# A hybrid decoder step on one core: another order for the pieces ahead of the feed-forward products, other weights with low parts by DMA, other preparation leads

## The chip, the core and the metric

The kernel runs on one core of a Trainium2 chip. The core has a TensorE (PE, matmuls; its weight loads are shown apart as PEld), a VectorE (DVE), a ScalarE (ACT), a GpSimd (POOL) and a SyncE (SP), which here only issues DMAs. The metric is the device time of one execution in microseconds (us), the median of several.

## The reference

One layer of a decoder trunk for 1024 prompt tokens and 8 sample tokens that share the weights, all in fp32. Two mixers share one input projection: a pooling mixer (means over trailing windows 2, 4, 8, 16) and a convolution mixer (gated, 31 taps, layer norm, swish). Then come cross attention over 256 memory tokens (the prompt makes keys and values, the samples read caches), SwiGLU and a final norm.

```python
def pool_mixer(a_ext, start_pos, w_map, b_map, scale):
    ...
        win_sum = cg[:, POOL_HIST + 1:] - cg[:, POOL_HIST + 1 - w: POOL_HIST + 1 - w + L]
        outs.append(win_sum / cnt - af[:, POOL_HIST:, sl])
    ...
def mem_kv(mem, g_mem, w_k, w_v):
    m = rmsnorm(mem, g_mem)
    k = (m @ w_k).reshape(B, N_MEM, MEM_HEADS, MEM_HEAD_DIM)
    v = (m @ w_v).reshape(B, N_MEM, MEM_HEADS, MEM_HEAD_DIM)
    return k, v
def layer(...):
    h = rmsnorm(x, g_mix)
    u = h @ w_in
    a = u[..., :POOL_WIDTH]
    val = u[..., POOL_WIDTH:POOL_WIDTH + CONV_CH]
    gate = u[..., POOL_WIDTH + CONV_CH:]
    glu = val * jax.nn.sigmoid(gate)
    ...
    x = x + jnp.concatenate([ya, yb], axis=-1) @ w_out
    x = x + cross_attn(rmsnorm(x, g_attn), mk, mv, w_q, w_o)
    h = rmsnorm(x, g_ffn)
    x = x + (jax.nn.silu(h @ w_gate) * (h @ w_up)) @ w_down
```

## The kernel before

**Tiling.** Everything is kept transposed: 1024 channels are 8 blocks of 128 partitions, and the 1032 tokens are the free dimension (even prompt tokens, odd ones, samples), cut in 3 chunks of 344 for matmuls. An fp32 product is three fp32r matmuls of high and low parts (`PASSES`), so every weight block and every operand is first split in two: high part = a rounded copy, low part = value minus high part.

**Splits.** `split` (L367) makes the high part on ACT (L375) or POOL (L377) and the low part by a subtraction on DVE or POOL (L386). `split_by_dma` (L392), used for the weight blocks that `BY_DMA` names, makes the high part on ACT (L397) or POOL (L399), writes its negative in the low part's place in the same way, and POOL issues a DMA that reads the weight block again from memory and adds it there (L404). A weight block is loaded to a `raw` slot by SP (L361; 3 slots), and its two parts go to a `w` slot or, for the names in `WIDE`, to an `op` slot. A weight's preparation is put in the plan as many blocks ahead of its use as `LEAD` says (`w_take`, L461).

**What sets the order.** The kernel's functions only record tasks: engines that could do it, a cost for each, tiles read and written. `Program.order` (L146) then lays them out once, when the program is built: again and again it issues the task that can start first by the planner's own costs, and among those that tie the one with the lowest number, if a slot is free in its pools (`op` 19 slots, `scr` 3, `raw` 3, PSUM `mm` and `ms` 2 each, and others). Each engine gets its instructions as one fixed queue. On the chip an engine then works through its queue, and waits where an input isn't there.

**The pieces.** The numbers of the tasks follow the string `ORDER` (L41) up to the last operands of the feed-forward products. A letter is a piece and the digit its part: `g`, `v` gate and value products of the convolution mixer, `A` input products of the pooling mixer, `C`, `D`, `s` the convolution's sums, `W` windows (L806: doubling sums L821 to L826, mean L833 to L835), `n`, `m` the memory's norm and split, `K` keys (L850, PSUM tile kps, copied by DVE as kf at L861), `V` values (L925, PSUM tile vps, copied by ACT as vf at L939), `M` the pooling mixer's map (L871, PSUM tile pmap, which waits for the window tile win and a free PSUM tile; its copy is yf, split to opa), `L` layer norm, `O` and `B` the two halves of the output projection (PSUM oa and ob, weights w_out_a and w_out_b), `t` squares, `q` queries, `S`, `T`, `P` scores, transposed probabilities (pT) and their products with values (pv, copied by DVE as oo, L1096) of the prompt's attention, `a` to `e` the samples' attention (sample scores ss at L1143 from DVE's products at L1130; qd and pd are their queries and probabilities, which go through memory), `o` its output projection (po), and `u`, `x`, `y`, `z`, `h`, `r`, `i`, `j` the second norm, the feed-forward operand blocks, and the first of its weights. Weights are loaded and prepared in the order in which these pieces take them.

**Behind the pieces** come the feed-forward products (22 tiles, PSUM tile pr, L1336), the last blocks (`fd`, L1678) and the final norm. In `BY_DMA` only `w_dn` and `w_dn2` belong to them.

## Time and profile before

| | us |
|---|---|
| median of 3 runs (lowest, highest) | 1222.66 (1222.16, 1227.87) |
| the profiled execution: its own time | 1224.5 |
| its span in the trace | 1222.6 |
| TensorE busy | 1198.6 |
| DVE busy | 931.0 |
| mean granted TensorE clock | 0.996 |

The span is the time from the first to the last recorded instruction; the execution's own time holds in addition what lies around it. In the rows that the prediction quotes, times are us from the span's start; a timeline row has start, length, engine, line, operation, tiles and shapes, and in brackets the idle time ahead of it with what ended it. "x6" is the number of instructions in the row.

Where pieces stand in the profiled execution: input products to about 148, keys and values from 148.30, layer norm behind 215, output projection, queries from 302, the prompt's and samples' attention to 453, its output projection from 452.96 and the feed-forward products from 544.

### The profile page before, as it was taken

Reading aid. Unit: us, or ns where it says so; the run is one execution under the profiler, and the core shown is the slowest. Engines: PE = TensorE matmul, PEld = TensorE weight load, DVE = VectorE, ACT = ScalarE, POOL = GpSimd, SP = SyncE. Lnnn points to the kernel's source line nnn. Section 1 sums busy time; section 2 is a strip of 40 time slices with the busy share of each in tenths; the row PEclk is TensorE's granted clock in tenths of the full one; section 3 lists DMA queues with packets and bytes.
Section 4 is the critical chain, followed back from the end, with each engine's and each line's share of the span. In section 5 each row is a group of like instructions: output and inputs, shape, how many; then the busy total and the mean of one; then the engine's idle time right before and its main releaser. Section 6 shows DMA issues by size and latency. Waiting matters only on the chain.

```text
span 1222.6 us, 19409 instructions
## 1 busy us (share of the span) xinstructions
PE 1198.6 (98%) x7720; PEld 1122.5 (92%) x7720; DVE 931.0 (76%) x1558; ACT 519.8 (43%) x712; POOL 248.1 (20%) x294
## 2 busy tenths in 40 slices
PE   7999999999999999999999999999999999999997
PEld 7999987999999979998999999999999999999886
DVE  7899998655359876679877787777867798889754
ACT  7665656354124543454222222232232355444533
POOL 3587761224101002122000000000000023331101
PEclk9999999999999999999999999999999999999999
DMA  7235567433475775531322232222313597678512
GB/s 287 68 73 125 133 213 238 130 112 131 156 264 177 236 264 174 139 104 53 130 103 74 110 116 105 100 83 105 122 70 104 195 317 222 168 191 224 142 48 92
DMA packets 60314, 180.21 MB, mean 147 GB/s; under 512 B 7808, under 2 KB 11584, under 8 KB 58944
## 3 DMA queue, kind: packets, MB, share of 16 engines
q1 hardware_dynamic: 53824, 157.92, 36.8%
q0 software_dynamic: 6400, 21.06, 9.6%
q8 instruction: 60, 0.98, 0.3%
q14 instruction: 30, 0.25, 0.1%
HBM read 145.18 MB, written 33.78 MB: 146 GB/s over the span
## 4 chain that ended last, share of the span: by engine, by line
PE 81%; DVE 10%; DMA 4%; issue 2%; ACT 2%; POOL 1%; SPq 0%; DVEq 0%; POOLq 0%; ACTq 0%
PE pr L1336 48%; PE po L487 7%; PE ps L487 7%; PE fd L1678 6%; PE oa L487 4%; PE ob L487 4%; DVE cacc L691 3%; POOL y L674 1%; PE sc L1033 1%; DVE spcache_k L1130 1%; PE psv L487 1%; PE psg L487 1%; DMA spcache_k<-in_cache_k 1%; DMA raw<-in_w_out_a 1%; DVE w L386 1%
## 5 line engine op out<-in xcount | busy, mean ns | idle before, releaser
L1336 PEld LDWEIGHTS pr<-ab,wTb 128*128 128x128 f32 x1056 | 132.2, 188 | 3.6
L1336 PE MATMUL pr<-ab,wTa 128*128 128x260 f32 x1056 | 133.7, 282 | 0.1
L1336 PE MATMUL pr<-ab,wTb 128*128 128x260 f32 x1056 | 133.4, 282 | 0.0
L1336 PEld LDWEIGHTS pr<-ab,wTa 128*128 128x128 f32 x1056 | 131.0, 188 | 2.3 <-DVE su L1352 0.3
L1336 PE MATMUL pr<-ab,wG 128*128 128x512 f32 x528 | 129.3, 393 | 0.0
L1352 DVE TENSOR_TENSOR su<-pr,su 128x520 f32<-128x520 f32 (+1 forms) x112 | 77.6, 694 | 58.0 <-PE pr L1336 57.8
L1336 PEld LDWEIGHTS pr<-ab,wG 128*128 128x128 f32 x528 | 96.2, 188 | 19.6 <-DVE wG L386 0.4
L487 PE MATMUL ps<-xop,w 128*128 128x344 f32 x720 | 114.1, 320 | 0.0
L487 PEld LDWEIGHTS ps<-xop,w 128*128 128x128 f32 x720 | 113.6, 188 | 0.0
L1336 PEld LDWEIGHTS pr<-hb,dV 128*128 128x128 f32 x768 | 98.5, 188 | 3.9
L1336 PE MATMUL pr<-hb,dV 128*128 128x260 f32 x768 | 99.7, 283 | 0.0
L487 PE MATMUL ps<-xq,w 128*128 128x344 f32 x576 | 94.7, 321 | 0.0
L487 PE MATMUL po<-oo,w 128*128 128x344 f32 x576 | 91.2, 320 | 0.0
L487 PEld LDWEIGHTS po<-oo,w 128*128 128x128 f32 x576 | 90.9, 188 | 0.2 <-issue 0.2
L487 PEld LDWEIGHTS ps<-xq,w 128*128 128x128 f32 x576 | 90.7, 188 | 0.1
L691 DVE SCALAR_TENSOR_TENSOR cacc<-glu,vec,cacc 128x511 f32<-128x511 f32 (+14 forms) x116 | 77.4, 737 | 0.0
L1336 PE MATMUL pr<-hb,dW 128*128 128x512 f32 x288 | 73.9, 393 | 0.0
L1678 PE MATMUL fd<-ho,w 128*128 128x260 f32 (+1 forms) x432 | 69.2, 321 | 1.0 <-DVE x L1352 1.0
L375 ACT ACTIVATE w<-raw 128x1024 fp32r<-128x1024 f32 (+1 forms) x34 | 31.9, 941 | 90.0 <-issue 28.1
L1678 PEld LDWEIGHTS fd<-ho,w 128*128 128x128 f32 x432 | 61.8, 188 | 8.2 <-issue 1.9
L1363 POOL MEMSET su<- 128x16 f32 x22 | 2.4, 111 | 319.9 <-PE pr L1336 268.6
L1336 PE MATMUL pr<-ab,wU 128*128 128x512 f32 x264 | 64.8, 394 | 0.0
(306 smaller groups left out, 2178.1 us busy)
## 6 DMA issues: line engine op xcount, KB each, us to landing
gr<-in_w_gu SPq DMA_DIRECT2D x44, 512.0 KB, 3.6
hb<-su SPq DMA_DIRECT2D x8, 1040.0 KB, 4.2
hs<-hb SPq DMA_DIRECT2D x16, 520.0 KB, 4.3
dr<-in_w_dn SPq DMA_DIRECT2D x16, 512.0 KB, 7.4
spcache_k<-in_cache_k SPq DMA_DIRECT2D x12, 512.0 KB, 4.0
hs<-hb SPq DMA_DIRECT2D x12, 512.0 KB, 7.8
raw<-in_w_in SPq DMA_DIRECT2D x10, 512.0 KB, 3.6
hb<-he SPq DMA_DIRECT2D x8, 520.0 KB, 3.8
```

The costliest lines, as they stand in the source:

```text
L375: e.activation(dst(0), src(), AF.Copy, scale=1.0 if gain is None else gain)
L386: e.tensor_tensor(dst(1), src(), f32(dst(0)), ALU.subtract)
L487: e.matmul(ps[:, c, :CW], w[:, wi, cols], x[:, xi, c * CW : (c + 1) * CW], start=first and p == 0, stop=last and p == 2)
L674: add({"Pool": pool_tt(HALF), "DVE": dve(HALF)}, lambda e: e.tensor_tensor(yb[:, i, HALF + n : SEQ], yb[:, i, HALF + n : SEQ], cp[:, q, : ...
L691: e.scalar_tensor_tensor(acc[h][:, n:], src[:, : HALF - n], w, acc[h][:, n:], ALU.mult, ALU.add)
L1033: e.matmul(bank()[:, i * NMEM : (i + 1) * NMEM], qop[2 * h + dt][:, qi, tt * P : (tt + 1) * P], kk[:, ki, 2 * (h % 2) + dt], start=(dt == ...
L1130: e.scalar_tensor_tensor(piece[:, b], piece[:, b], 1.0, bc[:, b], ALU.mult, ALU.mult, accum_out=out(m)[:, first + b : first + b + 1])
L1336: e.matmul(bank(c), w[:, wi, cols(j)], xs[0](j, xi)[:, c * n : (c + 1) * n], start=onto is None and j == 0 and p == 0, stop=j == nj - 1 an ...
L1352: from_sums(sums, "DVE", dve, lambda e, src, sl: e.tensor_tensor(as_banks(o(sl), src), src, as_banks(a(sl), src), op), [akey], [okey])
L1363: add({"Pool": 0.12}, lambda e: e.memset(o(), 0.0), [], keys)
L1678: e.matmul(view(i), w[:, wi, col : col + P], hops[k][:, xi, half, lo - half * HALF + i * width // count : lo - half * HALF + (i + 1) * wid ...
```

## The change

Three tables of constants are replaced: the order of the pieces, the weight blocks whose low part is made by DMA, and the leads. No function is changed.

```diff
 ORDER = (
-    "m0 m3 A3 n0 g1 v1 m5 g2 v2 m4 g3 s0 C0 C1 v3 m1 A0 A2 D0 s1 m2 A1 m7 m6 K0 K1 W3 V1 K2 W0 V0 s2 D1 W1 s3 W2 M0 M3 C2 "
...
+    "m1 m3 A3 m4 m5 n0 g1 g3 v1 m0 m7 g2 v2 m6 s0 C0 C1 v3 A0 A1 A2 D0 s1 m2 W3 K0 K1 V1 K2 W0 V0 D1 s2 C2 s3 W1 W2 M0 M3 "
...
 )
 
-BY_DMA = {"w_in": (4, 5, 7, 9, 10, 11), "w_k": (2, 3, 6), "w_o": (2, 4, 5, 6, 7), "w_out_a": (2, 3), "w_out_b": (0, 1), "w_q": (7,), "w_v": (0, 7), "w_dn": (17, 19), "w_dn2": (1,)}
+BY_DMA = {"w_in": (4, 5, 7, 9, 10, 11), "w_k": (2, 3, 6), "w_o": (4, 5, 6, 7), "w_out_a": (2, 3), "w_out_b": (1, 2), "w_q": (3, 5, 7), "w_v": (0, 7), "w_dn": (17,), "w_dn2": ()}
 WIDE = ("w_k", "w_v")
-LEAD = {"w_k": 2, "w_v": 2, "w_out_a": 15, "w_q": 13, "w_in": 1, "w_out_b": 11, "w_o": 9}
+LEAD = {"w_k": 3, "w_v": 1, "w_out_a": 16, "w_q": 15, "w_in": 2, "w_out_b": 13, "w_o": 10}
```

What it moves is seen in the engines' queues. In what follows a number behind a tile's name tells buffers of the same name apart, and differs between the two programs for the same tile. "x12" is the number of instructions of a row.

The first place is TensorE behind the first keys: the second pair of keys (kps), the values of columns 512 to 1023 (vps1, four weights of a quarter each) and the third pair of keys. Before:

```order
L857 MATMUL kps_1619<-memg_348,w_1464 128x256 x12
L857 MATMUL kps_1619<-memg_372,w_1464 128x256 x12
L857 MATMUL kps_1619<-memg_348,w_1482 128x256 x12
L857 MATMUL kps_1619<-memg_372,w_1482 128x256 x12
L934 MATMUL vps_1691<-w_1530,memg_348 128x512 x12
L934 MATMUL vps_1691<-w_1545,memg_348 128x512 x12
L934 MATMUL vps_1691<-w_1555,memg_372 128x512 x12
L934 MATMUL vps_1691<-w_1598,memg_372 128x512 x12
L857 MATMUL kps_1777<-memg_348,w_1662 128x256 x12
```

And now:

```order
L857 MATMUL kps_1615<-memg_348,w_1445 128x256 x12
L857 MATMUL kps_1615<-memg_372,w_1445 128x256 x12
L934 MATMUL vps_1649<-w_1529,memg_348 128x512 x12
L857 MATMUL kps_1615<-memg_348,w_1510 128x256 x12
L857 MATMUL kps_1615<-memg_372,w_1510 128x256 x12
L934 MATMUL vps_1649<-w_1545,memg_348 128x512 x12
L934 MATMUL vps_1649<-w_1560,memg_372 128x512 x12
L857 MATMUL kps_1754<-memg_348,w_1696 128x256 x3
L934 MATMUL vps_1649<-w_1660,memg_372 128x512 x12
L857 MATMUL kps_1754<-memg_348,w_1696 128x256 x9
```

The first quarter of vps1 has moved between the two weights of the second keys, and its last quarter into the third keys. What follows (the rest of these keys, pmap0, vps0, pmap3, pmap1, the last keys, pmap2) keeps its order.

The second place is POOL at the same time: the low parts by DMA of the second keys' two weights (`in_w_k`) and of the fourth quarter of vps1 (`in_w_v`), and the sums of a window tile (win). Before:

```order
L399 TENSOR_SCALAR w_1482<-raw_1250 128x1024
L404 DMA w_1464<-in_w_k 128x1024
L404 DMA w_1482<-in_w_k 128x1024
L821 COPY win_1514<-win_1514 128x2x4
L822 TENSOR_TENSOR win_1514<-win_1514 128x2x508
L386 TENSOR_TENSOR w_1545<-raw_1468,w_1545 128x1024
L386 TENSOR_TENSOR w_1555<-raw_1501,w_1555 128x1024
L386 TENSOR_TENSOR kT_1641<-kf_1626,kT_1641 128x512
L404 DMA w_1598<-in_w_v 128x1024
```

And now:

```order
L404 DMA w_1445<-in_w_k 128x1024
L824 COPY win_1480<-a_523 128x1
L825 TENSOR_TENSOR win_1480<-a_523 128x511
L826 TENSOR_TENSOR win_1480<-a_523 128x512
L821 COPY win_1480<-win_1480 128x2
L822 TENSOR_TENSOR win_1480<-win_1480 128x2x511
L821 COPY win_1480<-win_1480 128x2x2
L822 TENSOR_TENSOR win_1480<-win_1480 128x2x510
L821 COPY win_1480<-win_1480 128x2x4
L822 TENSOR_TENSOR win_1480<-win_1480 128x2x508
L404 DMA w_1510<-in_w_k 128x1024
L386 TENSOR_TENSOR w_1545<-raw_1453,w_1545 128x1024
```

All sums of window 3 are now POOL's and stand between the two DMAs; before, DVE did all but the last. The first sum of window 0 (L824 to L826) goes from DVE to POOL as well, a little further on, ahead of the DMA for the first low part of vps0's weights. In DVE's queue, ahead of the copy of the third keys, the low parts of one weight and of one value operand, and one product of the gating (L723), come in.

The third place is TensorE at the end of the attention: the sample scores of the last head (ss) and the prompt's products pv around them, written as pv with the transposed probabilities pT and the values vv. Before:

```order
L1091 MATMUL pv_4321<-pT_0_4195,vv_1806 128x512 x3
L1091 MATMUL pv_4321<-pT_1_4228,vv_1806 128x512 x3
L1143 MATMUL ss_4346<-ident,ssc 8x128 x2
L1091 MATMUL pv_4349<-pT_0_3804,vv_1987 128x512 x3
L1091 MATMUL pv_4349<-pT_1_3864,vv_1987 128x512 x3
```

And now:

```order
L1091 MATMUL pv_4346<-pT_0_3728,vv_1981 128x512 x3
L1091 MATMUL pv_4346<-pT_1_3835,vv_1981 128x512 x3
L1143 MATMUL ss_4369<-ident,ssc 8x128 x2
L1091 MATMUL pv_4374<-pT_0_4209,vv_1815 128x512 x3
L1091 MATMUL pv_4374<-pT_1_4220,vv_1815 128x512 x3
```

The scores stood between pv7 (here pv_4321) and pv0 (pv_4349) and now stand behind pv0 (now pv_4346), ahead of pv6. On SP's queue the last head's sample query (qd) goes ahead of two 1 MB loads of cached values at the same place. From the third of the feed-forward tiles on, all queues are as they were, up to two low parts of last blocks (`w_dn` 19, `w_dn2` 1) that DVE now makes.

8 rows, old and new, of the table ORDER are left out of this document.

## The prediction

> **What bounds the kernel now.** I read the page's busy line and its chain of waits first, to see which engine sets the end.
>
> ```profile
> PE 1198.6 (98%) x7720; PEld 1122.5 (92%) x7720; DVE 931.0 (76%) x1558; ACT 519.8 (43%) x712; POOL 248.1 (20%) x294
> PE 81%; DVE 10%; DMA 4%; issue 2%; ACT 2%; POOL 1%; SPq 0%; DVEq 0%; POOLq 0%; ACTq 0%
> ```
>
> TensorE is busy 1198.6 of 1222.6 us, and the change takes no matmul away: it can win only TensorE's idle time. So the second view is the busy time by stretch (start and end, length, then busy us of each engine, granted clock, DMA share, GB/s).
>
> ```profile
> 0.00:20.00 20.00, 13.34 (x71) 12.53 (x72) 11.68 (x16) 13.01 (x18) 6.99 (x44) 1.00 0.88 316
> 20.00:160.00 140.00, 139.97 (x905) 138.56 (x904) 134.45 (x198) 89.29 (x118) 95.57 (x75) 1.00 0.43 114
> 160.00:180.00 20.00, 18.53 (x102) 15.52 (x100) 19.93 (x32) 11.06 (x14) 12.57 (x7) 1.00 0.79 240
> 180.00:200.00 20.00, 16.81 (x63) 12.52 (x64) 19.48 (x34) 13.98 (x16) 1.76 (x2) 0.91 0.76 223
> 200.00:360.00 160.00, 160.00 (x1017) 156.95 (x1016) 89.01 (x129) 60.46 (x63) 37.27 (x21) 1.00 0.49 161
> 420.00:440.00 20.00, 18.75 (x121) 16.01 (x120) 17.78 (x53) 13.19 (x34) 1.68 (x6) 1.00 0.59 193
> 440.00:460.00 20.00, 18.89 (x95) 16.13 (x96) 15.26 (x58) 5.72 (x12) 0.97 (x4) 1.00 0.99 367
> 1140.00:1222.60 82.60, 73.58 (x478) 66.41 (x476) 40.89 (x70) 35.49 (x59) 8.54 (x11) 0.96 0.31 91
> ```
>
> The start (6.66 us idle, mostly the first weight's load) and the end (9.02) lie outside the reordered pieces. Within them the idle sums to 1.47 + 3.19 + 1.25 + 1.11 = 7.0 us, and 180–200 also ran at a clock of 0.91, worth about 16.81 x 0.09 = 1.5 us. **The ceiling of the change is about 8.5 us.** Who is waited for in the larger of the two places, the view of TensorE's waits says (total, times, longest); the two smaller waits stand with the attention below.
>
> ```profile
> PE pmap L877 <- ACT vf L939: 2.9, 1, 2.9
> PE vps L934 <- DVE kf L861: 1.7, 1, 1.7
> ```
>
> **The layer-norm end of the mixers (160–200), where the gain is.** First rows of the timeline, with the load as the chain of waits has it and, last, the windows view of 196 to 200:
>
> ```profile
> 170.89 5.90 PE L857 MATMUL kps<-memg,w 128*128 128x256 f32 x48
> 176.63 1.90 PE L877 MATMUL pmap<-win,wmap 128*128 128x344 f32 x6
> 179.51 0.68 DVE L861 TENSOR_TENSOR kf<-kps,side 128x512 f32<-128x512 f32 x1
> 180.24 11.35 PE L934 MATMUL vps<-w,memg 128*128 128x512 f32 x48 [1.72 <-DVE kf L861]
> 183.09 8.80 DMA raw<-in_w_out_a
> 191.43 1.90 PE L877 MATMUL pmap<-win,wmap 128*128 128x344 f32 x6
> 191.97 1.06 ACT L397 ACTIVATE w<-raw 128x1024 fp32r<-128x1024 f32 x1 [3.54 <-DMA raw<-in_w_out_a]
> 193.55 1.23 DVE L835 SCALAR_TENSOR_TENSOR win<-win,a 128x1032 f32<-128x1032 f32 x1
> 194.98 1.25 ACT L939 ACTIVATE vf<-vps,rmc 128x512 f32<-128x512 f32 x2
> 196.28 3.62 PE L877 MATMUL pmap<-win,wmap 128*128 128x344 f32 x6 [2.94 <-ACT vf L939]
> 196.00:200.00 4.00, 3.72 (x9) 2.44 (x10) 3.78 (x5) 3.50 (x5) 0.00 (x0) 0.57 0.98 220
> ```
>
> First wait: the keys kps2 end at 176.8, but DVE, full to the brim (19.93 of 20 us), reaches their copy kf2 only at 179.51; values vps0 need that buffer. The change takes from DVE, ahead of kf2, window 3's first three sums and window 0's first one.
>
> ```profile
> L825 DVE TENSOR_TENSOR win<-a x4: 677/680/684, 144.7 to 192.1; 128x511 f32<-128x511 f32 x4
> L822 DVE TENSOR_TENSOR win<-win x5: 1212/1215/1219, 146.6 to 198.6; 128x1022 f32<-128x1022 f32 x3, 128x1020 f32<-128x1020 f32 x2
> 188.39 0.15 DVE L824 COPY win<-a 128x1 f32<-128x1 f32 x1
> 187.25 1.22 DVE L386 TENSOR_TENSOR w<-raw,w 128x1024 fp32r<-128x1024 f32 x1
> ```
>
> Four halves at 0.68, two whole sums at 1.21 and four copies of 0.15 are 5.7 us less. Coming in ahead of kf2 are two low parts (L386, 1.22 each) and one product of full width (L723, 1.2 by the same size); one convolution sum leaves (half as wide, 0.7). Net 5.7 - 3.6 + 0.7 = 2.8 us: kf2 could start at 176.7, so it starts when kps2 ends, about 176.85. vps0 follows pmap0 at once, 178.5 instead of 180.24: **1.7 us**.
>
> Second wait: pmap1 waits for the PSUM buffer of vps0, so for ACT's vf0, and ACT stands at the high part of a weight whose load took 8.80 us; from it to vf0 are 194.98 - 191.97 = 3.0 us of two passes over the weight and one part of opa, and vf0 takes 1.25. That load starts when its slot is released by a low part that DVE makes behind kf2; with DVE some 2 us earlier it starts at about 181.
>
> ```profile
> raw<-in_w_out_a SPq DMA_DIRECT2D x4, 512.0 KB, 3.6
> ```
>
> Such loads took 3.6 us in the median of the four (the view of DMA issues), the one that counts 8.80. I take 7 us, near the longer end, because the queue is as full there as before but two loads that stood ahead of it now start earlier; the bounds are the two rows. Then ACT starts the high part at 188, and vf0 is done at 188 + 3.0 + 1.25 = 192.3, vps0 having ended near 189.8. The other input, window 1's mean, ended at 194.78; DVE has 2.6 us less ahead of it, less 0.6 for kf2 now waiting for its keys: about 193.0. This is what is late next. pmap1 starts at 193.0 instead of 196.28. pmap3, 1.7 earlier with vps0, ends at 191.6, so that the gap is 1.4 us, not 2.94.
>
> That length matters: six pmap matmuls took 1.90 us in two rows above, but 3.62 behind the 2.94 us gap, where the granted clock is 0.57 on average over 196–200, while the 1.72 us gap ahead of vps0 was followed by 11.35 us at full rate. So the half clock goes too (about **1.6 us**): kps3 starts near 194.6 instead of 199.37, and the whole place gives **4.8 us**. The Trainium skill, page "TensorE: Matmul & The Clock Gate", Part 1, has the clock halve only after an idle window of about 3.4 us that runs freely; here 2.94 us sufficed. By the page a gap that stays near 3 us might cost nothing more than itself, which would make the first rival below milder by that 1.6; the row decides.
>
> **What the low parts by DMA may take back.** The accumulate DMAs (L404) were priced by their landing.
>
> ```profile
> DMA to landing us min/median/max: 6.5/8.3/9.0
> DMA to landing us min/median/max: 5.5/7.8/11.1
> 142.66 0.88 POOL L404 DMA_DIRECT2D w<-in_w_k  x1 [1.52 <-ACT w L397]
> 144.82 0.87 POOL L404 DMA_DIRECT2D w<-in_w_k  x1 [1.28 <-ACT w L397]
> 158.63 0.88 POOL L404 DMA_DIRECT2D w<-in_w_v  x1
> 171.93 0.88 POOL L404 DMA_DIRECT2D w<-in_w_v  x1
> 150.46 1.88 POOL L822 TENSOR_TENSOR win<-win 128x1016 f32<-128x1016 f32 x1
> ```
>
> The first row is that of 130–260, the second of 360–560. Window 3 now stands on POOL between the two DMAs of kps1's weights: three sums of 1.88, two halves of 0.95 and four copies of 0.19 are 8.3 us. From 142 the second DMA so moves from 144.82 to 150–152; landed 8.3 later, 158–160 (bounds 156.5 and 161). Its products would have stood at 157, but a quarter of vps1 now goes between them, so they are wanted at 159.9. vps1's last low part, issued near 159, lands at 167.3 against a need at 168.8; vps0's first one, near 171, at 179.3 against 178.5, but pmap1 waits for window 1 until 193.0 anyway, so up to 1.5 us of that is hidden. Further on w_out_b 1 and 2 take the place of 0 and 1, and w_q 3 and 5 join 7, each with 0 to 3 us to spare. I take 0.8 us for all; bounds: 0, and six of them late by the 2.8 between 8.3 and 11.1, 17 us. The near end, since TensorE never stopped for a low part by DMA before. The Trainium skill's "DMA: Bandwidth & Descriptors", on the anatomy of a DMA, would price such a transfer at 2.0 us plus its 512 KB at 436 GB/s, an estimate of 3.2 us; then nothing would be taken back and the sum would be 0.8 us better. The rows say 8.3, more than twice that, so the page is not used.
>
> **Attention (380–600).** The sample scores ss3 now come behind pv0 instead of ahead of it.
>
> ```profile
> 439.99 5.82 PE L1091 MATMUL pv<-pT,vv 128*128 128x512 f32 x24 [1.06 <-DVE oo L1096]
> 446.69 0.27 PE L1143 MATMUL ss<-ident,ssc 128*8 128x128 f32 x1 [0.78 <-DVE spcache_k L1130]
> 447.29 5.83 PE L1091 MATMUL pv<-pT,vv 128*128 128x512 f32 x24 [0.33 <-DVE oo L1096]
> 452.96 12.23 PE L487 MATMUL po<-oo,w 128*128 128x344 f32 x76
> ```
>
> The 0.78 is covered by pv0, 2.9 us as half of the 5.83; part of the 0.33 stays, and the 1.06 ahead of pv3 too, since its evacuation on DVE (oo) stands behind the same sums as before. I take **1.0 us**; the bounds are 0 (the sample loads set it, under the 367 GB/s of 440–460) and the 2.2 of all three. Behind ss3 hang the last sample softmax, its sums over the cached values and the last two inputs of the first output products; those products run 12.23 us in one piece behind pv6 before TensorE would wait for them, so 2.9 us later costs nothing. On SP's queue the query of the last head is now issued ahead of two 1 MB loads of cached values, which works against a later ss3.
>
> **Nothing** I give the rest: other leads and pieces between 200 and 360 move under a TensorE busy 160.00 of 160, and two low parts of last blocks that go from POOL's DMA to DVE (2 x 1.22 us) fall where DVE works 40.89 of 82.60 us; uncovered they cost 2.4. From the third gated tile to 1147 us every engine's order is as it was.
>
> Sum: 4.8 + 1.0 - 0.8 = 5.0 us. The profiled execution took 1224.5 (span 1222.6 and 1.9 around it) and becomes 1219.5; it lies 1.8 above the median 1222.66, so the **forecast is 1217.6**.
>
> **The rivals.** (a) *The wait stays with the load.* If the 8.80 us repeat from 181.2, the high part waits until 190.0, vf0 is done at 190 + 3.0 + 1.25 = 194.3, and pmap1's gap is 194.3 - 191.6 = 2.7 us, near enough to 2.94 to keep the half clock. Only 2.0 us are won there; 2.0 + 1.0 - 0.8 = 2.2 makes **1220.5**. For it: a DMA share of 0.76 in that stretch; against it: the two loads ahead of it go out earlier.
>
> (b) *All gaps close:* 8.5 us, **1214.2**. For it: no gap is longer than 3 us and each has one cause; against it: the cause of pv3's isn't touched.
>
> (c) *Slower: low parts come late.* POOL has to finish window 3 before it issues kps1's second low part; if that is later than reckoned, or the transfers take the 11.1 us seen instead of 8.3, TensorE stops inside kps1, at vps1's end and ahead of vps0, and again at w_out_b and w_q. Three stops of 2.8, one half clock (1.6) and two more stops of 2.8 are 15.6; less the 5.8 won elsewhere that is 9.8 slower, **1232**. Two stops (5.6) already eat the gain; from there on it decides the sign. For it: margins of 0 to 3 us at six places; against it: POOL worked only 12.57 of 20 us in 160–180, no row of the waits names L404, and a stop gives the next transfer time.
>
> (d) *The order changes and the end doesn't.* The time freed on DVE is taken by work that moves up, vps0's earlier start only lengthens the gap of pmap1, and the sum over 160–200 stays at 4.7 us idle and one half clock: **1222**. For it: DVE stays full either way; against it: what moves up (low parts, one product) is the 3.6 us already charged.
>
> **How the numbers follow.** Forecast 0.40, (a) 0.15, (b) 0.17, (c) 0.18, (d) 0.10. The forecast's own range is 1215.5 to 1220, from the load's bounds and those of the low parts. The range reaches one microsecond below (b), 1213, and upwards past (a) and (d) to 1227, where three stops without the later two would end; that leaves out most of (c) and a little below, 0.19. A measurement of this kernel tells 0.5%, 6.1 us, from no change: below 1216.55 and above 1228.8. Faster: (b) and 0.16 of the forecast's 0.40, 0.33; slower: (c) but for its mild part, 0.15; the same: the rest, 0.52.
>
> **What would show it.** Right: vps0 starting within 0.3 us of pmap0's end near 178.5; pmap1 lasting 1.9 us at clock 1.00; kps3 near 194.6; no wait of ss for spcache_k. Wrong: waits of kps, vps, ob or ps for L404 or a weight; a granted clock under 1 anywhere between 150 and 600; a pmap gap of 3 us again.

## The result, and the profile after

| | before | after |
|---|---|---|
| median (lowest to highest; 18 runs each) | 1223.68 (1221.53 to 1227.87) us | 1229.44 (1225.56 to 1235.59) us |
| ratio, with its 95% interval | | 1.0048 [1.0037, 1.0059] |
| the profiled execution, its span | 1224.5, 1222.6 us | 1233.62, 1231.8 us |
| TensorE busy | 1198.6 us | 1203.3 us |

The changed kernel is 5.8 us slower, where 5.0 us were forecast as a gain. The view by stretch (start and end, length, busy us of PE, PEld, DVE, ACT, POOL, granted clock, DMA share, GB/s) shows two of the stretches that were shown of before:

```profile
20.00:160.00 140.00, 136.53 (x856) 134.91 (x855) 131.74 (x183) 87.09 (x114) 93.75 (x77) 0.98 0.43 101
160.00:180.00 20.00, 18.03 (x95) 15.47 (x94) 19.97 (x32) 9.78 (x11) 13.62 (x10) 0.91 0.79 213
```

TensorE's matmuls are the same 7720; it is busy 4.7 us longer because more of them ran at a lower granted clock (0.98 and 0.91 in these rows). The first surprise is the stretch 20 to 160: 3.5 us idle and a clock of 0.98, where before it was busy 139.97 of 140.00 at 1.00. The view of TensorE's waits of the changed kernel (us in total, times, longest) names the places:

```profile
PE Rx_ps L517 <- DVE Rx_m L519: 3.5, 1, 3.5
PE pmap L877 <- ACT opa L375: 3.0, 1, 3.0
PE vps L934 <- DVE kf L861: 2.0, 1, 2.0
...
PE ss L1143 <- DVE spcache_k L1130: 0.5, 2, 0.2
```

No low part by DMA (L404) is among them. Three places carry the time: one at 32 us that the prediction didn't look at, the keys and values, and the attention.

**At 32 us.** The timeline of the changed kernel (start, length, engine, line, tiles, in brackets the wait ahead):

```profile
31.04 1.13 POOL L377 TENSOR_SCALAR w<-raw 128x1024 fp32r<-128x1024 f32 x1 [4.12 <-PE psv L487]
32.25 2.39 POOL L386 TENSOR_TENSOR w<-raw,w 128x1024 fp32r<-128x1024 f32 x1
32.36 3.36 DVE L386 TENSOR_TENSOR w<-raw,w 128x1024 fp32r<-128x1024 f32 x1
36.38 0.59 PE L517 MATMUL Rx_ps<-xss,ones_d 128*128 128x8 f32 x2 [3.47 <-DVE Rx_m L519]
```

and that of the kernel before at the same place:

```profile
31.61 1.22 DVE L386 TENSOR_TENSOR w<-raw,w 128x1024 fp32r<-128x1024 f32 x1
31.82 1.91 POOL L377 TENSOR_SCALAR w<-raw 128x1024 fp32r<-128x1024 f32 x1 [4.88 <-PE psv L487]
```

DVE's low part takes 1.22 us when it starts ahead of POOL's high part, and then it is POOL that is stretched (1.91). When POOL is 0.8 us earlier, POOL's own low part runs first, DVE's starts 0.11 us behind it and takes 3.36, the operand norm behind it is late, and TensorE stands 3.47 us and then works at half clock for a while: the first keys start at 153.65 instead of 148.30. The engines' queues up to this point are word for word the same in both kernels, so it is not the new order that made this. It is a race between two engines whose outcome differs from execution to execution; the runs below show the loss with the old queues, too, and a smaller one of 1.2 us.

**Keys and values.** What the second place of the change became, in the changed kernel's timeline:

```profile
153.65 8.78 PE L857 MATMUL kps<-memg,w 128*128 128x256 f32 x72
156.93 2.69 POOL L386 TENSOR_TENSOR w<-raw,w 128x1024 fp32r<-128x1024 f32 x1
156.94 0.75 DVE L691 SCALAR_TENSOR_TENSOR cacc<-glu,vec,cacc 128x510 f32<-128x510 f32 x1
157.59 2.08 DVE L813 COPY side<-a 128x8 f32<-128x8 f32 x1
162.41 1.23 DVE L835 SCALAR_TENSOR_TENSOR win<-win,a 128x1032 f32<-128x1032 f32 x1
163.56 0.68 DVE L861 TENSOR_TENSOR kf<-kps,side 128x512 f32<-128x512 f32 x1
164.40 4.58 PE L934 MATMUL vps<-w,memg 128*128 128x512 f32 x12 [1.97 <-DVE kf L861]
186.29 0.68 DVE L861 TENSOR_TENSOR kf<-kps,side 128x512 f32<-128x512 f32 x1
203.33 1.97 PE L877 MATMUL pmap<-win,wmap 128*128 128x344 f32 x6 [2.96 <-ACT opa L375]
```

and in that of the kernel before:

```profile
148.30 11.63 PE L857 MATMUL kps<-memg,w 128*128 128x256 f32 x96
151.86 0.51 DVE L813 COPY side<-a 128x8 f32<-128x8 f32 x1
155.56 0.68 DVE L861 TENSOR_TENSOR kf<-kps,side 128x512 f32<-128x512 f32 x1
159.76 11.29 PE L934 MATMUL vps<-w,memg 128*128 128x512 f32 x48
```

Before, vps1 started 11.5 us behind the first keys, and the buffer that it takes was freed by kf0 (the copy of the first keys) at 7.3 + 0.7 us, long ahead. Now its first quarter should start 8.8 us behind them, between the two weights of the second keys, and kf0 comes only at 9.9 (163.56 - 153.65): ahead of it in DVE's queue stand a weight's low part and window 3's mean (L835), whose sums are ready earlier now that POOL makes them, and a copy of 128x8 that takes 2.08 us under POOL's low part. TensorE waits 1.97 us, and twelve matmuls take 4.58 us. Further on come the two waits that the forecast was about. vps0 has no wait for kf2 in this profile, but not because kf2 is earlier: it starts at 186.29, which is 32.6 us behind the first keys, and before it was 31.2 (179.51 - 148.30). TensorE has merely come later itself: pmap0, ahead of vps0, starts at 185.74 and takes 1.90 us. And pmap1 still waits 2.96 us. Its row names an operation of ACT, but window 1's mean, which it reads, ends in the same profile at 203.18, just ahead of it, and vf0 at 199.93, long ahead.

**Attention.** In the changed kernel's timeline behind 423:

```profile
423.28 1.15 POOL L399 TENSOR_SCALAR w<-raw 128x1024 fp32r<-128x1024 f32 x1 [12.54 <-PE ps L487]
423.44 1.26 DVE L1130 SCALAR_TENSOR_TENSOR spcache_k<-spcache_k,sbcache_k 128x256 f32<-128x256 f32 x1
425.17 1.03 ACT L1011 ACTIVATE qo<-ps 128x1032 fp32r<-128x1032 f32 x1 [1.01 <-DVE qs L1014]
427.68 1.65 PE L1091 MATMUL pv<-pT,vv 128*128 128x512 f32 x6 [1.23 <-ACT oo L1095]
```

A new wait: DVE's product takes 1.26 us beside POOL's operation (its neighbours in the queue take 0.42), ACT's query copy waits 1.01 us behind it, and the copy of pv (at 427.04) stands behind that and behind the second pass (1.05 us) of a w_o block whose low part goes by DMA.

The stages of the executions that were profiled, from the starts of the first matmuls of each tile in the timeline (kps, oa, queries, po), in us; "race" is the wait of Rx_ps for Rx_m:

| kernel | race | first keys at | first keys to output projection | queries to po | own time |
|---|---|---|---|---|---|
| before | none | 148.3 | 58.6 | 150.8 | 1224.5 |
| after | 3.5 | 153.6 | 59.7 | 154.1 | 1233.6 |
| after, once more | none | 148.2 | 60.6 | 152.4 | 1227.0 |
| old head, new tail | 3.5 | 152.8 | 56.8 | 152.3 | 1228.7 |
| new head, old tail | 1.2 | 149.2 | 60.7 | 151.3 | 1226.8 |
| before, race cured (two runs) | 0.5, 0.2 | 148.2, 148.1 | 57.1, 56.9 | 151.3, 150.7 | 1223.3, 1222.2 |
| after, race cured | none | 148.2 | 60.2 | 151.5 | 1225.8 |
| new order alone, race cured | 0.5 | 148.1 | 59.7 | 153.1 | 1226.5 |
| new weights and leads alone | 1.2 | 149.5 | 59.2 | 154.1 | 1230.3 |

From the first keys to the output projection the four profiles with the old head (order, weights and leads of before) take 56.8 to 58.6 us, the four with the whole new head 59.7 to 60.7. The 58.6 are the execution from which the forecast was read: there pmap1 waited 2.94 us and six matmuls behind it took 3.62. In the other three, with the same queues in this stretch, pmap1 waited 1.64 us (`tail_after`), 0.86 and 1.60 (`before_rx`), and the six took 1.97 to 2.00. So part of what was to be won there was the bad luck of one execution.

### The profile page after: what moved, and what is told of

It reads as the page before. It is cut to its first block, busy times and chain, and to the rows that moved or that the text cites. A ratio compares the mean times of both kernels' runs of the same rounds, so it can differ in the third digit from the quotient of the medians.

```text
span 1231.8 us, 19416 instructions
## 1 busy us (share of the span) xinstructions
PE 1203.3 (98%) x7720; PEld 1126.4 (91%) x7720; DVE 937.7 (76%) x1549; ACT 518.6 (42%) x710; POOL 257.3 (21%) x304
## 4 chain that ended last, share of the span: by engine, by line
PE 75%; DVE 14%; DMA 5%; issue 3%; ACT 1%; SPq 0%; POOL 0%; DVEq 0%; ACTq 0%; POOLq 0%
PE pr L1336 46%; PE po L487 7%; PE fd L1678 6%; DVE cacc L691 4%; PE ps L487 4%; PE oa L487 4%; PE ob L487 4%; PE vps L934 2%; DVE spcache_k L1130 1%; DMA hs<-hb 1%; DMA sbcache_v<-pd 1%; DVE w L386 1%; DVE spcache_v L1130 1%; PE pv L1091 1%; PE kps L857 1%
```

## The experiments

Times are medians with lowest and highest; ratios are to the kernel before, run on the same chip in turn, with their 95% intervals.

**Two halves of the change.** `head_after` has the new order, weights and leads up to the last squares (t7) ahead of the queries and the old ones behind, `tail_after` the other way round:

```diff
 ORDER = (
-    "m0 m3 A3 n0 g1 v1 m5 g2 v2 ... t6 t7 q0 q1 a0 b0 f0 c0 ..."
+    "m1 m3 A3 m4 m5 n0 g1 g3 v1 ... t6 t7 q0 q1 a0 b0 f0 c0 ..."
```

> The changed order, low parts by DMA and leads up to the squares of the output projection's result (t7), and the old ones from the queries (q0) on. Three places lost time in the changed kernel's profile: the wait of Rx_ps for Rx_m (32 to 37 us), vps1 behind kf0 (160 to 180 us), and the attention (400 to 460 us). Theory A (each place has its own cause, and the first is chance, since the queues are equal word for word up to there): this kernel keeps the kf0 wait and loses the attention's part; against before +0 to +2.5 us, 1224 to 1226. Theory B (the loss is all in the head, attention only follows): +5 to +6, 1229 to 1230. Theory C (all in the tail): 0 or a gain of up to 1.

> The other half: old order, low parts and leads up to t7, the changed ones from q0 on. Theory A: the attention's stops return (3 us more TensorE idle over 400 to 460 than before's), +2.5 to +4 us, 1226 to 1228, and kps, vps, pmap run as before. Theory B: within 1 us of before. Theory C: the whole +5.8.

Measured: `head_after` 1226.89 us (1224.6 to 1233.41), ratio 1.003 [1.0016, 1.0045]; `tail_after` 1224.42 us (1223.47 to 1229.02), ratio 1.0007 [0.9994, 1.002]. Most of the lasting loss sits in the head, 3.0 us; the interval of the tail alone reaches from 0.7 us won to 2.5 lost. No theory fits as it was stated: A expected less of the head and more of the tail, B more of the head. In the profiled execution of `tail_after`, whose head is that of before, the race was lost as well; its timeline:

```profile
32.42 3.36 DVE L382 TENSOR_TENSOR w<-raw,w 128x1024 fp32r<-128x1024 f32 x1
```

TensorE waits 3.47 us behind it. So the old queues lose it too, with the same numbers.

**The race cured,** in both kernels, by keeping the fourth weight block's two parts off POOL:

```diff
+            if i == 3:
+                state["alone"] = True
             split(lambda p: w[:, p], lambda p: (w, p), lambda: raw[:], 1024, [(raw,)])
+            if i == 3:
+                state["alone"] = False
```

> The kernel before, with the two parts of the fourth weight block (raw3) made by ACT and DVE instead of POOL, so that POOL works on nothing while DVE makes the low part ahead of Rx_m. If POOL's operations hold up DVE's by chance there, this removes the chance: no Rx_ps wait over 1.5 us in the profile, the runs spread less than before's 1221.5 to 1227.9, and the median falls by the share of runs that had it times up to 5 us: 0 to -2.5 us. If the wait at 32 us in the changed kernel was due to the change, nothing happens here: within 1 us of before, same spread.

> The changed kernel with the same edit. Chance theory: the 3.5 us wait and the half clock behind it go; the median falls from 1229.4 by 1 to 5 us and the spread (1225.6 to 1235.6) shrinks to under 6 us. If the wait comes from the change itself (by DMA traffic or by ACT): it stays over 2 us in the profile and the median stays within 1 us of 1229.4.

Measured: `before_rx` 1223.62 us (1222.01 to 1224.71), ratio 0.9996 [0.9986, 1.0005]; `after_rx` 1226.99 us (1225.45 to 1229.17), ratio 1.0022 [1.0011, 1.0033]. The spread of the changed kernel shrinks from 10.0 to 3.7 us. What is left between the cured kernels, run on one chip in turn, is 3.4 us; this is the change's own. The rest of the 5.8, some 2.4, is put down to the race. That is argued from the times, since only one execution of each run has a trace: 16 of the 18 times of the changed kernel in the first comparison lie above 1228.5 us, and 2 of 12 with the race cured. The kernel before gains nothing clear by the cure. The stage table agrees: first keys to output projection 57.0 before and 60.2 after. The timeline of `after_rx` at the second place:

```profile
148.17 8.78 PE L861 MATMUL kps<-memg,w 128*128 128x256 f32 x72
158.14 0.68 DVE L865 TENSOR_TENSOR kf<-kps,side 128x512 f32<-128x512 f32 x1
158.97 3.03 PE L938 MATMUL vps<-w,memg 128*128 128x512 f32 x12 [2.02 <-DVE kf L865]
176.09 1.25 DVE L837 TENSOR_TENSOR win<-win,cnt 128x16 f32<-128x16 f32 x1
180.88 0.68 DVE L865 TENSOR_TENSOR kf<-kps,side 128x512 f32<-128x512 f32 x1
181.61 1.20 PE L938 MATMUL vps<-w,memg 128*128 128x512 f32 x4 [0.67 <-DVE kf L865]
196.44 1.23 DVE L839 SCALAR_TENSOR_TENSOR win<-win,a 128x1032 f32<-128x1032 f32 x1
197.82 2.65 PE L881 MATMUL pmap<-win,wmap 128*128 128x344 f32 x6 [2.00 <-DVE win L839]
```

kf0 again at 10.0 us and a wait of 2.02, so this doesn't hang on the race; here the matmuls behind it run at full rate. kf2 comes 32.7 us behind the first keys (180.88 - 148.17), where the two profiles of `before_rx` have 31.3, and vps0 does wait for it, 0.67 us. pmap1 waits for window 1's mean, which ends at 197.67.

**The early quarter, and window 3's sums.** `after_rx_seq` puts vps1 back behind the second keys, `after_rx_win3dve` gives DVE window 3's sums back, and `before_rx_win3pool` makes in the kernel before a step on which the forecast rested: all of window 3's sums on POOL.

```diff
-                add({"PE": pe(512, 6)}, emit, wkeys + [(memg[k // 4], p, k % 4) for p in range(2)], [(ps,)])
+                add({"PE": pe(512, 6)}, emit, wkeys + [(memg[k // 4], p, k % 4) for p in range(2)] + [("kdone", c)], [(ps,), ("vdone", c)])
```

```diff
-            add({"Pool": pool_tt(SEQ) + 0.1, "DVE": dve(SEQ) + 0.08}, emit, [ck], [nk], lock=True)
+            add({"Pool": pool_tt(SEQ) + 0.1} if g in (3,) else {"Pool": pool_tt(SEQ) + 0.1, "DVE": dve(SEQ) + 0.08}, emit, [ck], [nk], lock=True)
```

> The changed kernel with the POOL edit of the fourth weight block, and vps1 put back behind the whole of kps1 and ahead of kps2 (TensorE's order of before there); of the other queues nearly nothing moves. Theory K (the head loses time because vps1's first quarter comes 3 us earlier than before and has to wait for the buffer that DVE frees with kf0, about 2 us plus a half clock in some runs): that wait goes, and 2 to 3.5 us of the 3.4 that the changed kernel with the POOL edit is slower than before come back, 1223.5 to 1225. My prediction's steps behind it (kf2 in time, pmap1 early) would then show as up to 4.8 us more, down to 1220. Theory D (DVE has no time to give, the window sums on POOL hold it up or are replaced by other work): the wait moves to kf2 or to pmap1 and the time stays at 1226 to 1228.

> The changed kernel with the POOL edit and window 3's sums kept on DVE (the planner then also puts vps0 ahead of pmap0). If the sums on POOL are what hurts (POOL holding DVE up, low parts by DMA late behind them): faster than the changed kernel with the POOL edit (1227.0) by 2 to 4. If they do relieve DVE as the prediction counted, 5.7 us of sums come back on DVE, kf2 waits again and pmap1 longer: slower by 1 to 3.

> The kernel before with the POOL edit and all of window 3's sums on POOL: the prediction's step by itself, with the old order, low parts and leads. If DVE is relieved by 4 us as counted, kf2 comes in time and pmap1's gap shrinks: 3 to 4.8 us faster than before with the POOL edit (1223.6), 1219 to 1221. If POOL's work costs DVE as much as it takes off (theory D): within 1 us of 1223.6, or slower by up to 3 where the low parts by DMA come late.

Measured: 1230.74 us (1227.05 to 1233.3), ratio 1.0051 [1.0032, 1.0069]; 1229.38 us (1227.06 to 1231.48), ratio 1.0042 [1.0026, 1.0057]; 1230.73 us (1228.16 to 1231.23), ratio 1.0048 [1.0034, 1.0062]. All three are slower than the kernels they start from, by 2 to 7 us. With vps1 back in its place its last low part is late (timeline of `after_rx_seq`):

```profile
171.10 2.12 PE L938 MATMUL vps<-w,memg 128*128 128x512 f32 x8 [2.26 <-DMA w<-in_w_v]
```

This is the lateness that rival (c) spoke of: the early quarter in the changed kernel makes room for the DMA behind window 3's sums. And the forecast's step in `before_rx_win3pool`:

```profile
179.76 1.10 PE L938 MATMUL vps<-w,memg 128*128 128x512 f32 x4
198.56 6.34 PE L881 MATMUL pmap<-win,wmap 128*128 128x344 f32 x12 [5.13 <-ACT vf L943]
```

vps0 has no wait for kf2 any more, as reckoned, and starts at 179.76; but vps1 waits 1.46 us for its low part ahead of that, pmap1 5.13 behind it, and the kernel is some 7 us slower than `before_rx`. The planner laid out everything behind anew in these three (here pmap0 stands behind vps0), so none of them shows its step alone. `after_rx_win3dve` is slower by what the forecast's counting would have it, with the sums back on DVE.

**Which table.** `no_order` has the new weights by DMA and leads with the old order; `order_only_rx` the new order with the old weights and leads, the race cured.

> The changed low parts by DMA and leads with the old order of pieces. If the loss comes from these two tables alone: +3 to +6 us on before. If from the order's interleaving: within 1.5 us of before.

> The new order of pieces alone, with the weights by DMA and the leads of before, and the loss at 32 us taken away. Here the first quarter of vps1 stands right behind the first keys, and the second keys need the buffer that kf0 frees; ahead of kf0 DVE has two low parts and window 3's mean. Theory (the early quarter and DVE's queue ahead of kf0 make the loss, whatever the tables of weights): kps1 waits for kf0 1 to 2 us behind that quarter, the stretch from the first keys to the output projection takes 59 to 62 us, and the time is 1226 to 1231. Rival (the loss comes from the weights by DMA and the leads): the stretch is back at 57 to 58 us, and the time at 1223 to 1225.

Measured: `no_order` 1230.63 us (1225.77 to 1236.03), ratio 1.0048 [1.0031, 1.0065]; `order_only_rx` 1226.31 us (1224.3 to 1229.24), ratio 1.0014 [1.0001, 1.0027]. The new weights and leads with the old order are 6.6 us slower, but here the race is not cured, and the times spread over 10 us, so how much of this is theirs isn't separated; in the profiled execution 1.2 us are the race's, and the stage from the queries to po is 3.2 us longer than before. The new order alone costs 2.1 us against the kernel before on the same chip, 2.7 against `before_rx` on another. Its timeline:

```profile
157.38 5.99 PE L861 MATMUL kps<-memg,w 128*128 128x256 f32 x48 [0.55 <-DVE kf L865]
193.38 5.43 PE L881 MATMUL pmap<-win,wmap 128*128 128x344 f32 x12 [2.59 <-ACT vf L943]
207.84 8.33 PE L491 MATMUL oa<-opa,w 128*128 128x344 f32 x51 [1.55 <-DVE kf L865]
```

The stretch is 59.7 us, as expected of the order, but the wait for kf0 is 0.55 us and not 1 to 2: the loss has moved on, to pmap (2.59, with a half clock: twelve matmuls in 5.43 us where six take 1.90) and to oa (1.55). So the order makes the loss in this stretch, but not by the wait for kf0 alone.

**Single waits taken away.** `after_rx_kf0` moves kf0 four tasks up in DVE's queue once the order is made, `after_rx_kf02` kf2 as well, `before_rx_kf2` kf2 in the kernel before; nothing else moves.

```diff
+        for t, n in self.ahead:
+            ...
+            issued = rest + [(u, "DVE") for u in moved] + issued[i + 1 :]
...
-        add({"DVE": dve(512)}, lambda e: e.tensor_tensor(
+        copy = add({"DVE": dve(512)}, lambda e: e.tensor_tensor(
...
+        pg.ahead.append((copy, {0: 4}.get(q, 0)))
```

> The changed kernel with the POOL edit, and in DVE's queue alone one instruction moved: the copy kf0 goes six places up, ahead of a weight's low part and window 3's mean. All other queues are the same word for word. Theory S (the head's loss is that copy standing too late for the place to which the change moved vps1): the 2.0 us wait of vps1 falls under 0.5 and no half clock follows it; 1.5 to 3.5 us come back, 1223.5 to 1225.5, against 1227.0 without the move. Theory D (DVE is the bound of the whole stretch up to the layer norm, so what vps1 gains, kf2 and pmap1 wait longer): 1226 to 1227.5, with pmap1's gap longer by what vps1's lost.

> The same, and kf2 six places up as well. Theory S: 0.5 us better than with kf0 alone. Theory D: no difference beyond 0.5 us.

> The kernel before with the POOL edit, and in DVE's queue alone kf2 four places up, ahead of four convolution sums: the gap that my prediction wanted to win, by the smallest edit. Theory S: vps0 starts 1.8 us earlier, from the first keys to the output projection 55.3 to 56.8 us instead of 57.1 to 58.6; 1221 to 1222.5, and so faster than before. Theory D: vps0 starts earlier, but pmap1 then waits that much longer for vf0 or its window; within 0.7 us of 1223.6.

Measured: 1229.84 us (1228.9 to 1231.02), ratio 1.0045 [1.0032, 1.0058]; 1231.07 us (1229.39 to 1233.78), ratio 1.0054 [1.0042, 1.0066]; 1227.15 us (1225.11 to 1229.19), ratio 1.002 [1.0008, 1.0032]. Each takes its wait away and loses 3 to 4 us to the cured kernel that it starts from, which neither theory allowed for. The timeline of `after_rx_kf0`:

```profile
170.19 0.47 PE L875 MATMUL kps<-memg,w 128*128 128x256 f32 x2 [1.66 <-DVE kf L879]
171.68 0.58 PE L875 MATMUL kps<-memg,w 128*128 128x256 f32 x1 [1.02 <-POOL w L400]
200.72 1.77 PE L896 MATMUL pmap<-win,wmap 128*128 128x344 f32 x4 [3.29 <-DVE win L853]
```

vps1 starts without a wait (at 156.79), and the 2.02 us come back at the third keys, which wait 1.66 for the copy of the second and 1.02 for a weight's low part by POOL, and as 3.29 instead of 2.00 at pmap1. In `before_rx_kf2` vps0 starts at 178.17 with no wait, near the 178.5 of the prediction, and pmap1 then waits 6.51 us for vf0. (The profile is of the slowest of its executions, 1229.19 us, so the usual gap may be smaller.) The chain of waits in that kernel says why:

```profile
184.39 9.15 DMA raw<-in_w_out_a
...
193.63 1.06 ACT w L411
...
197.93 3.81 PE pmap L896 x6
```

The load ends at 193.5, where before it ended at 183.09 + 8.80 = 191.9, although vps0 is 2 us earlier, and ACT does nothing for vf0 (196.73 to 197.89) until it has split that weight.

`before_rx_ahead` moves kf2, window 1's mean and vf0 up together:

```diff
+        pg.ahead.append((done, {1: 2}.get(g, 0)))
+        pg.ahead.append((copy, {2: 4}.get(q, 0)))
+            pg.ahead.append((copy, {0: 3}.get(c, 0)))
```

> The kernel before with the POOL edit, and three operations moved up in their own engine's queue: kf2 by four places (DVE), window 1's mean by one task (DVE), and vf0 by three (ACT), ahead of the two passes over a weight whose load it otherwise waits behind. If pmap1's gap is due to vf0's place behind that load, as its 6.5 us in the run with kf2 alone say: vps0 starts 1.8 us earlier, pmap1's gap falls from 6.5 to 1 to 2, and the stretch is 53.5 to 55.5 us instead of 57; 1220.5 to 1222, faster than both kernels. If the load itself binds TensorE elsewhere (kps3's or oa's weights late): the wait moves there, and it is not faster than 1223.

Measured: 1224.87 us (1222.54 to 1228.33), ratio 1.0011 [1.0, 1.0023]. The gap ahead of pmap1 is 6.48 us still, in a profile that is again of the slowest execution. On ACT vf0 still stands behind one pass over a w_out_a block, and now DVE stands at the same load too: its queue holds a low part of that weight ahead of window 1's second sum (view of its timeline):

```profile
194.00 1.23 DVE L405 TENSOR_TENSOR w<-raw,w 128x1024 fp32r<-128x1024 f32 x1 [3.25 <-ACT w L394]
196.77 1.23 DVE L858 SCALAR_TENSOR_TENSOR win<-win,a 128x1032 f32<-128x1032 f32 x1
```

**Less work for DVE.** Eight of the sums (cacc) of the convolution's fourth group are left out, some 5.2 us of DVE's rows ahead of kf2; the output is then that of fewer taps.

```diff
         def tap(e, h, n):
+            if cg == 3 and 5 <= n <= 8:
+                return
```

> The kernel before with the POOL edit, leaving out 8 of the 31 taps of the fourth convolution group (DVE, 8 x 0.65 = 5.2 us between the copies kf0 and kf1); every other instruction and every queue the same. If DVE bounds the stretch from the first keys to the output projection: 3 to 4.5 us shorter there (57 to 53 or 54), vps0 without a wait for kf2 and pmap1's gap under 1 us; 1219.5 to 1221. If the weight loads and ACT behind them bound it: vps0 starts 1.8 us earlier but pmap1 waits that much longer for vf0; within 1.5 us of 1223.7, or slower as with kf2 moved alone.

> The changed kernel with the POOL edit, leaving out the same 8 taps (here they stand around kf0 and kf1). DVE as the bound: the stretch falls from 60.2 to 56 to 57.5 us, 1222.5 to 1224.5. Loads as the bound: within 1.5 us of 1227.0.

Measured: `before_rx_taps` 1222.51 us (1220.7 to 1226.34), ratio 0.9987 [0.9973, 1.0]; `after_rx_taps` 1229.38 us (1227.05 to 1230.6), ratio 1.0037 [1.0022, 1.0052]. In the kernel before, that is worth about 1.1 us (the page has DVE busy 927.8 us against 930.4 in `before_rx_2`, so half of the 5.2 came back as longer operations); its timeline:

```profile
179.25 11.32 PE L940 MATMUL vps<-w,memg 128*128 128x512 f32 x48 [0.89 <-DVE kf L867]
193.94 1.97 PE L883 MATMUL pmap<-win,wmap 128*128 128x344 f32 x6 [1.62 <-DVE win L841]
```

The wait for kf2 falls only from 1.82 to 0.89 us, and that of pmap1 is not shorter (0.86 and 1.60 in the two profiles of `before_rx`). In the changed kernel less work on DVE makes it some 2 us slower, and kf2 starts at 183.50 instead of 180.88, although all queues but for these sums are the same. So the amount of DVE's work alone doesn't set the length of this stretch.

**Attention.** `after_rx_pv` lets both halves of a pv tile end before either is copied:

```diff
+            both = [(ps, 0), (ps, 1)]
...
-                [(ps, c), (oo, 0, c)], [(oo, 1, c)])
+                both + [(oo, 0, c)], [(oo, 1, c)])
```

> The changed kernel with the POOL edit, and the two halves of each pv product kept ahead of the first half's evacuation in the plan (in the changed order pv1 and pv4 are split, and the second half waits for the first one's evacuation by ACT). Order only in the attention changes, by what the planner makes of it. If the split is what costs there: no wait of pv for ACT's oo, the stretch from the queries to po 150 to 151 us instead of 151.6, 1.0 us faster, 1225.5 to 1226.5. If not: the same time within 0.7, with another wait in its place.

Measured: 1232.95 us (1231.04 to 1234.38), ratio 1.007 [1.0055, 1.0086], some 6 us slower than `after_rx`, where a gain or no difference was expected. The wait of pv for ACT's copy is gone and others are larger: the waits view has pv for DVE's oo at 2.7 us in all (1.3 in `after_rx`), po for oo at 1.3. Between the two profiled executions 3.4 us are lost from the queries to po, 3.1 behind po and 1.2 in the head, whose queues are the same.

**Repeats.** `before_rx_2` is `before_rx` again, `after_again` the changed kernel itself.

> The kernel before with the POOL edit once more, as the base of the third run on the same chip: 1223 to 1224.5, with a spread under 4 us; the three waits at 176 to 200 us as before.

> The changed kernel once more, to see how the loss at 32 us is spread over its executions. Theory: it is lost in some executions and not in others, and an execution in which it is lost takes about 5 us more. Then, if the profiled execution has the wait of Rx_ps for Rx_m at 3.5 us, its time lies above 1229; if the wait is 0.5 us or none, the time lies at 1225 to 1228.5; and the times of the other executions spread over some 6 us or more. Rival: what makes the changed kernel slower than its version with the parts on other engines isn't this wait: then a profiled execution without it still takes over 1230, or one with it under 1228.

Measured: `before_rx_2` 1223.71 us (1222.23 to 1227.35), ratio 0.9994 [0.9985, 1.0004]. `after_again` 1227.01 us (1225.27 to 1232.38), ratio 1.0028 [1.0014, 1.0043]; its profiled execution took 1226.99 us. Its timeline at 32 us and at the second place:

```profile
31.53 1.22 DVE L386 TENSOR_TENSOR w<-raw,w 128x1024 fp32r<-128x1024 f32 x1
159.07 4.51 PE L934 MATMUL vps<-w,memg 128*128 128x512 f32 x12 [2.06 <-DVE kf L861]
199.23 1.97 PE L877 MATMUL pmap<-win,wmap 128*128 128x344 f32 x6 [3.50 <-DVE win L835]
```

The same program without the loss at 32 us (VectorE's low part in 1.22 us) took 1226.99 us, with it 1233.62: the profiled pair that the theory asked for, with the wait for kf0 unchanged (2.06 and 1.97). By the times, this comparison had fewer executions with the loss (4 of 12 above 1228.5 us), and the ratio is 1.0028 instead of 1.0048.

No version was clearly faster than the kernel before. `before_rx` has its median, and in its first run a spread of 2.7 us where the kernel before had 6.6 on the same chip. But in its second run the spread is 5.1 us, against 4.4 of the kernel before and under 4 expected, so it isn't shown that the cure steadies the kernel before.

## Why the prediction was wrong

**The layer-norm place (forecast: 4.8 us won; measured: about 3 lost, 60.2 against 57.0 us in the cured kernels).** The step that failed is "Net 5.7 - 3.6 + 0.7 = 2.8 us: kf2 could start at 176.7", with all that was built on it: vps0 at 178.5, window 1's mean at "about 193.0" and a gap of 1.4 us ahead of pmap1. In `after_rx` kf2 starts at 180.88, later than before and not earlier, vps0 at 181.61, and the mean ends at 197.67. The gap of pmap1 is 2.00 us there, 2.96 and 3.50 in the two profiles of the changed kernel as it is. What the runs showed in its place:

- *DVE's operations became longer.* The counting itself was right. If each operation ahead of kf2 is taken at the shortest time that its form shows in ten of these profiles, DVE's work there is 2.8 us less in `after_rx` than in `before_rx` (174.2 against 177.0). But some operations take longer than that, every one of those over 0.15 us beside an operation of POOL, and they add up to 8.4 us in `after_rx` against 4.1 and 3.7 in the two profiles of `before_rx`. The largest near the place are the copy of 128x8 (2.10 us for 0.17) and window 0's product with its counts (1.25 for 0.17). That POOL does these sums was priced at nothing for DVE, and this hold-up is more than the relief. This is worked out from the records of DVE; no run takes POOL's work out of this stretch.
- *A wait was put at nothing.* The first quarter of vps1 was seen to move 3 us forward, and only its weight was followed, never the buffer that it takes. kf0, which frees it, went from 7.3 to 9.9 us behind the first keys, and TensorE waits 1.97 to 2.06 us in each of the three profiles of the changed kernel. A low part and window 3's mean, which comes early because POOL now makes the sums, stand ahead of it by the order; the held copy is a third cause.
- *A shorter wait ahead of vps0 was taken for time won.* Where kf2 alone was moved in the kernel before, vps0 started at 178.17 and the kernel still lost 3.4 us: the load of w_out_a came no earlier (to 193.5, where before it ended at 191.9), and ACT stands at it ahead of vf0. The prediction had this load as its open size (3.6 to 8.8 us), and in these edited kernels it took 9.15 and 9.23. In the changed kernel it is not what binds: on the chains of `after_rx` and `after_again` it took 5.0 us, less than the 7 that were reckoned, and pmap1 waits for window 1's mean.

The half clock behind pmap1's gap did go in the changed kernel as it is (1.97 us for six matmuls), but not for the reason given: the gap stayed at 2.96 and 3.50 us; in `after_rx` the six took 2.65 behind 2.00. And the lower end of the forecast's own range, 1215.5, doesn't follow from the bounds of the load: by the same working pmap1 waits for window 1's mean until 193.0 however early the load ends.

Of the rivals, (d), that the time freed on DVE is taken up and the end doesn't move, comes nearest: nearly every wait that was removed came back at the next place. It was given 0.10 and 1222 us; the sum is off even so, since the changed kernel and most experiments lose 2 to 7 us rather than nothing. Even without the race the changed kernel would be 3.4 us slower, so the forecast didn't fail by the race alone.

**The low parts by DMA (0.8 us taken back).** No row of the changed kernel's waits names one, so the term was about right there. `after_rx` has one of 0.96 us within vps0, where up to 1.5 was reckoned as hidden, and pmap1 waits for its window behind it. The margins are as thin as rival (c) feared: with vps1 moved back one is 2.26 us late. With the old order the same tables are 6.6 us slower (`no_order` against 1224.06 for the kernel before beside it), but there only 0.3 us of TensorE's waits name a low part, and part of the loss may be the race.

**Attention (1.0 us won; measured 0.5 to 3.3 lost).** The wait of ss for spcache_k did shrink, from 0.78 us to two of 0.2, as forecast. (The size it started from varies: 1.4 and 0.6 in the two profiles of `before_rx`.) The new wait for ACT's copy (1.23) wasn't looked for: a POOL operation that holds DVE, and a pass of a w_o block on ACT ahead of the copy. From queries to po it is 151.5 against 151.0 us in the cured kernels, and 152.4 to 154.1 against 150.8 in the others.

**Nothing for the rest** held: behind po the three profiles of the changed kernel are 0.4 to 0.75 us shorter than that of before.

**The race at 32 us** was in no term and in no rival. Its cost, some 5 us an execution, is as large as the whole forecast. That the kernel before's slowest shown run stood 5.2 us above its median was there to be seen. Why the changed kernel lost it more often in the first comparison, if the times are read rightly, is open: the queues are the same up to there, and the repeat had it less.

**What stays open:** what the stretch from first keys to output projection is bound by in the end. It was shown that no single wait, and not the amount of DVE's work, sets it; that POOL's hold on DVE does it in the changed kernel, and the load of w_out_a with ACT and DVE behind it in the kernel before with kf2 moved, is argued from sums and chains. Neither a stretch without POOL's work beside DVE nor vf0 and window 1's second sum ahead of that weight's parts was tried.

## What to carry to other kernels

Where four engines are nearly full and each works through a fixed queue, an order of pieces is a balance: follow every instruction that moves earlier to the buffer that it takes and to the engine that frees it, and not only the wait that one hopes to remove. Work that goes to an engine which holds up the one it leaves has to be priced on both. A wait that is removed counts as won only when the next thing that its engine needs is known to be there. Before a difference of 5 us is put down to a change, look for a place where the profile differs though the queues don't.

## What the runs showed of the hardware

- *VectorE is held by GpSimd for some operations.* A subtraction of two tiles in on-chip memory, 1.22 us alone, took 3.36 when it started 0.11 us behind GpSimd's subtraction, and so ended 1.08 us after it: it hardly moved meanwhile. A copy of 128x8 took 2.08 us (0.17 in `before_rx_win3pool`, where the GpSimd operation beside it ended 0.03 us behind its start; 0.51 in the kernel before), and a product of the attention 1.26 instead of 0.42, while a sum that accumulates in PSUM (cacc) went through in 0.75 beside the GpSimd operation that held the copy. It holds the other way too: GpSimd's high part took 1.91 beside VectorE's low part, 1.13 alone. In these rows the subtraction that started first took its usual time (2.39 us on GpSimd, 1.22 on VectorE).
- *The half clock follows gaps of about 2 us in some executions and not in others.* Twelve matmuls behind gaps of 1.97 and 2.06 us took 4.58 and 4.51 us, behind one of 2.02 us 3.03; six behind 2.96 and 3.50 us took 1.97, where before 2.94 us were followed by 3.62. The length of a gap alone doesn't decide it, so the 1.6 us that the prediction won back with it is a size that no single profile gives.
